# Two-block transformer on one core: softmax divided after the product with the values, and layer norms summed in groups

## The chip, the cores and the metric

One core of a Trainium2 chip runs the whole program in one launch. The metric is the device time in microseconds (us). The engines are named as in the profile: PE (TensorE, matrix products), DVE (VectorE), ACT (ScalarE), POOL (GpSimd) and SP (it issues the DMAs). PE works at one of two clock levels, 2.4 GHz (granted clock 1.0) or 1.2 GHz (0.5).

## What is computed

Two blocks follow each other on 512 positions of width 1024, each with two layers. The first block has feed-forward parts, a windowed attention and a recurrent mixer; the change leaves its attention alone. The second block has, in layer 0, multi-head latent attention ("MLA", 16 heads) and, in layer 1, neighbourhood attention ("NA", 16 heads). A stream of 256 context positions runs its own MLA beside the main one. All of it is float32. Cut to what matters:

```python
def layer_norm(x, g, b):
    mu = jnp.mean(x, -1, keepdims=True)
    var = jnp.mean(jnp.square(x - mu), -1, keepdims=True)
    return (x - mu) * lax.rsqrt(var + LN_EPS) * g + b

def dense_attention(...):          # MLA, per head and block of queries
    s = jnp.concatenate([q_ctx @ k_ctx, q_lat @ k_lat], -1)
    p = softmax_f32(s * scale)
    return p[..., :n_ctx] @ v_ctx + p[..., n_ctx:] @ v_lat
# NA: the same with a window of latent keys, a bias, and all context keys

h_lat = layer_norm(DEEPNORM_ALPHA * h_lat + g1 * y, ln1_g[i], ln1_b[i])   # after attention
h_lat = layer_norm(DEEPNORM_ALPHA * h_lat + g2 * f, ln2_g[i], ln2_b[i])   # after the feed-forward part
```

## The kernel before

The stream lies transposed: eight tiles `x[0]` to `x[7]` of 128 features by 512 positions. Each float32 factor of a big product is split into a high and a low part (`split`: an ACT copy and a DVE subtraction), and a product is three matmuls (`mm3`). Weights arrive by DMA as `wr` and are split into `wh` (ACT) and `wl` (DVE).

The order of the instructions is not the order of the Python text. All calls go to a `Recorder`; its `schedule` is a list scheduler that knows a cost for each operation and, engine by engine, picks the earliest recorded operation that is ready, within a look-ahead of 1400 operations. The whole program is then emitted in that order, one in-order queue for each engine. `run` mixes the context stream into the main one by a share of the planned PE time, and the modulation products (`mr`) by spare planned DVE time.

**Attention before.** `attend` (MLA) handles one head and 256 queries: scores to PSUM, the maximum, then the exponentials on ACT, which also add up the denominators `den`. DVE takes the reciprocal of the two columns of `den`, and POOL multiplies every weight tile by it through `times`: `pc` (two halves of 128x256, context keys) and, in the main stream, `pl` (two tiles of 128x512, latent keys). The function `output`, which `Lag` holds back by two units, transposes the weights on PE, splits them and multiplies them with the values. Then ACT and DVE put the two 64-row parts of the result together in `out` (tile `os`), which holds two heads; after the second head (`e` = 1) it is split into `yh`, `yl` for the output projection. There are 32 such units in the main stream (16 pairs of heads) and 16 in the context stream (8 pairs). The unit of `na` is a pair of heads on half the queries, 16 units: four reciprocals in one DVE instruction, four `times` on tiles `P` of 128x512, and later `na_out`.

**Norms before.** `ln_part` norms 256 positions at a time. `colsum` adds the eight tiles with `total` (seven additions in two chains) and then sums over the partitions by a matmul with ones for each 128 positions. The sums of `x` are added on POOL, those of the squares `sq` on DVE. Then come mean, variance, the row broadcasts by transposes (`ident,c`) and the scaling. `ln_part` runs ten times: twice for the context, twice (two halves) after each of MLA, feed-forward 0, NA and feed-forward 1. Of the latter the first half runs beside other PE work and the second half ends the stage.

In the trace the stages of the second block lie at about 2067 to 2370 us (MLA units), 2370 to 2400 (its norm), 2400 to 2815 (feed-forward 0), 2860 to 3192 (NA and its norm), 3192 to 3539 (feed-forward 1) and from 3539 on the last norm. The context MLA lies at 908 to 1350 us, inside the first block. Nearly all instructions carry line 446, which is the emitter's; they are told apart by their tiles.

Of the kernel before, what the change touches and what calls it, by code (L numbers as in the profile page):

```python
# [16 lines left out]
ALU = mybir.AluOpType  # L17
# [44 lines left out]
FIRST = (100, 16)  # L62
HEAVY = 0.5
FILL, DEBT, STEP = 0.7, 5000.0, 500.0
FIRST_POOL = (1, 3)
# [405 lines left out]
class Core:  # L471
# [254 lines left out]

    def colsum(self, tiles, T, eng=None, more=0):
        nc = self.nc
        acc = self.total(tiles, T, eng)
        st = self.ps()  # L730
        for j in range(T // P):
            nc.tensor.matmul(st[:, j:j + 1], acc[:, j * P:(j + 1) * P], self.ones, start=True, stop=True)
        n = T // P
        return st[:, :n] if not more else tuple(st[:, i * n:(i + 1) * n] for i in range(more + 1))
# [14 lines left out]
    def bcast(self, col, T, copy=None):  # L749
        bc = self.ps()  # L750
        for j in range(T // P):
            self.nc.tensor.transpose(bc[:, j * P:(j + 1) * P], col[:, j:j + 1].to_broadcast([P, P]), self.ident)
        if copy is None:
            return bc[:, :T]
        self.nc.scalar.copy(copy[:, :T], bc[:, :T])
        return copy[:, :T]

    def times(self, p, c):
# [453 lines left out]
    def ln_part(self, xs, T, l, which, kind, mod, perm=False):  # L1212
# [8 lines left out]
        def part(sl):  # L1221
# [9 lines left out]
            for a in x:  # L1231
                q = self.t(s="sq")[:, :C]
                nc.scalar.activation(q, a, AF.Square)
                sq.append(q)
            s1 = self.colsum(x, C, nc.gpsimd)
            s2, v, q = self.colsum(sq, C, more=2)
            mu, m2 = self.col(n), self.col(n)
# [60 lines left out]

    def attend(self, qs, kl, kc, vs, c0, yrow, e, scale, out):
        nc = self.nc  # L1300
# [19 lines left out]
        for j in range(2):  # L1320
            js = slice(j * 256, (j + 1) * 256)
            nc.scalar.activation(pc[:, js], sc[:, js], AF.Exp, bias=nm[:, j:j + 1], scale=scale, accum_out=den[:, j:j + 1])
            if nl:
                nc.scalar.activation(pl[j], pl[j], AF.Exp, bias=nm[:, j:j + 1], scale=scale, accum_out=den[:, 2 + j:3 + j])
        if nl:
            nc.vector.tensor_tensor(den[:, 0:2], den[:, 0:2], den[:, 2:4], op=ALU.add)
        nc.vector.reciprocal(den[:, 0:2], den[:, 0:2])
        for j in range(2):
            self.times(pc[:, j * 256:(j + 1) * 256], den[:, j:j + 1])
            if nl:  # L1330
                self.times(pl[j], den[:, j:j + 1])

        def output():
            o = self.ps("turn")[:, :256]
            prev = None
            for k2 in range(1 + nl // 2):
# [12 lines left out]
                prev = (k2, pt)  # L1349
            apply(o, *prev)  # L1350
            nc.scalar.copy(out[r], o[low])
            nc.vector.tensor_tensor(out[r], out[r], o[r], op=ALU.add)
            if e:
                self.split(out, [a[:, c0:c0 + 256] for a in yrow])

        def apply(o, k2, pt):
            for i in range(2):
                v = vs[0][i] if k2 == 0 else vs[1][(k2 - 1) * 2 + i]
                nc.group()
                for part, a in enumerate(pt):  # L1360
# [54 lines left out]
    def mla(self, a_lat, x, kind, ctx_only, ctx_kv, after):  # L1415
# [26 lines left out]
        for qd in range(4):  # L1442
# [16 lines left out]
            for pr in range(2):  # L1459
# [26 lines left out]
                for sl in parts(T):  # L1486
                    both = self.t(s="os")[:, :256]
                    for e in range(2):
                        vs = [[v[(hp % 4) // 2][:, ((hp % 2) * 2 + e) * P:((hp % 2) * 2 + e + 1) * P] for v in vt] for vt in vts]
                        yield from lag.add(self.attend(qs[e], kbl[e] if kbl else None, kbc[e], vs, sl.start, y, e, scale, both))  # L1490
                    if qd == 3 and pr:
                        yield from lag.add(lambda out=out, sl=sl: out(sl))
# [92 lines left out]

    def na_out(self, pts, vctx, vband, y, half):
        nc = self.nc
# [30 lines left out]
        for e in range(2):  # L1618
            rr = rows[e]
            nc.vector.tensor_tensor(ts[rr].rearrange("p (j q) -> p j q", j=2).sized(256), ts[rr].rearrange("p (j q) -> p j q", j=2),  # L1620
                                    o[rr].rearrange("p (j e q) -> p e j q", j=2, e=2)[:, e], op=ALU.add)
        src = ts.rearrange("p (c r) -> p c r", r=GRID_R)
        hv, lv = (b.rearrange("p (r c) -> p c r", c=GRID_W)[:, 32 * half:32 * half + 32, :].sized(256) for b in y)
# [3 lines left out]
    def na(self, x, a, after):  # L1627
# [11 lines left out]
        for pr in range(8):  # L1639
# [30 lines left out]
            for half in range(2):  # L1670
                pts = [[], []]
                den = self.col(4)
                for jj in range(2):
# [24 lines left out]
                yield from lag.add(lambda pts=pts, vctx=vctx, vband=vband, y=y, half=half: self.na_out(pts, vctx, vband, y, half))  # L1698
            ys.append(y)
# [142 lines left out]
```

## Time and profile before

| | |
|---|---|
| time, median of 3 runs | 3553.25 us (3552.89 to 3555.09) |
| the profiled execution | 3556.54 us |
| span of the profiled execution | 3554.8 us |
| PE busy | 3463.3 us (97%) |
| DVE busy | 2668.0 us (75%) |
| ACT busy | 1811.8 us (51%) |
| POOL busy | 768.6 us (22%) |
| chain that ended last | PE 88%, DVE 5%, ACT 3%, DMA 2% |

The profile is of one execution. Busy time is the union of the instructions' spans; a queued instruction can start before the one ahead has written its last element, so spans overlap. A wait is read from the idle time of an engine and from what released it. The chain that ended last is PE's in nearly all of the program: time is lost where PE is idle, and gained or spent where PE's own work changes.

### The profile page before, as it was taken

How to read it: one execution, taken by the hardware profiler on the slowest of the kernel's cores; microseconds unless marked ns; L12 is line 12 of the kernel's file. 1: busy time of each engine (PE TensorE's matmuls, PEld its weight loads, DVE VectorE, ACT ScalarE, POOL GpSimd, SP SyncE). 2: the span in 40 equal slices, each digit the busy share in tenths (PEclk: the TensorE clock that was granted, in tenths of full speed). 3: DMA queues.
4: the chain of work that ended last, by engine and by line, in shares of the span. 5: the costliest groups of instructions: out<-in, count | busy, mean ns of one | idle time of the engine just before them, and what ended most of it. 6: DMA issues, size and time to landing. Idle time of an engine off the chain costs nothing.

```text
span 3554.8 us, 56919 instructions
## 1 busy us (share of the span) xinstructions
PE 3463.3 (97%) x19814; PEld 3046.3 (86%) x19814; DVE 2668.0 (75%) x5556; ACT 1811.8 (51%) x3933; POOL 768.6 (22%) x848
## 2 busy tenths in 40 slices
PE   6999999999999999999999999999999999989998
PEld 5888989888988889898888988888888889988887
DVE  8984689867697658798645699987668767876566
ACT  6443555534555455664333487874445444454333
POOL 4330032322132112223100133350001522240002
PEclk9999999999999999999999999999999999999999
DMA  9874145556376542448535212124343143333330
GB/s 337 293 229 123 58 151 155 184 159 191 104 252 193 163 119 93 117 146 268 180 104 150 87 44 60 57 69 130 106 127 107 54 125 104 91 105 104 97 90 24
DMA packets 276448, 475.37 MB, mean 134 GB/s; under 512 B 40000, under 2 KB 55872, under 8 KB 276160
## 3 DMA queue, kind: packets, MB, share of 16 engines
q1 hardware_dynamic: 276160, 471.74, 43.4%
q8 instruction: 156, 2.56, 0.3%
q14 instruction: 132, 1.08, 0.1%
HBM read 448.81 MB, written 5.50 MB: 128 GB/s over the span
## 4 chain that ended last, share of the span: by engine, by line
PE 88%; DVE 5%; ACT 3%; DMA 2%; issue 1%; POOL 0%; SPq 0%; POOLq 0%; DVEq 0%; ACTq 0%
PE ps L446 88%; DVE wl L446 1%; ACT L446 1%; DVE c L446 0%; DVE x L446 0%; DVE pl L446 0%; ACT pth L446 0%; ACT pl L446 0%; SPq L446 0%; DMA mr<-in_wmod 0%; DVE ptl L446 0%; ACT gt L446 0%; DMA wr<-in_dn 0%; DVE mr L446 0%; ACT pc L446 0%
## 5 line engine op out<-in xcount | busy, mean ns | idle before, releaser
L446 DVE TENSOR_TENSOR wl<-wr,wh 128x512 fp32r<-128x512 f32 (+1 forms) x1182 | 851.9, 741 | 136.8 <-ACT wh L446 100.7
L446 ACT CAST wh<-wr 128x512 fp32r<-128x512 f32 (+1 forms) x1182 | 678.5, 614 | 116.6 <-PE ps L446 65.5
L446 PE MATMUL ps<-hh,wh 128*128 128x512 f32 (+1 forms) x1864 | 687.7, 369 | 4.9 <-ACT hh L446 4.8
L446 PE MATMUL ps<-hh,wl 128*128 128x512 f32 (+1 forms) x1864 | 684.5, 367 | 6.0 <-DVE wl L446 6.0
L446 PE MATMUL ps<-hl,wh 128*128 128x512 f32 (+1 forms) x1864 | 685.4, 368 | 4.4 <-DVE hl L446 4.4
L446 PE MATMUL ps<-fh,wh 128*128 128x512 f32 (+1 forms) x1344 | 464.1, 345 | 0.0
L446 PE MATMUL ps<-fl,wh 128*128 128x512 f32 (+1 forms) x1344 | 461.8, 344 | 0.0
L446 PE MATMUL ps<-fh,wl 128*128 128x512 f32 (+1 forms) x1344 | 461.7, 344 | 0.0
L446 PEld LDWEIGHTS ps<-hh,wl 128*128 128x128 f32 x1864 | 352.2, 189 | 65.6 <-DVE wl L446 7.8
L446 PEld LDWEIGHTS ps<-hh,wh 128*128 128x128 f32 x1864 | 352.6, 189 | 61.7 <-ACT hh L446 5.8
L446 PEld LDWEIGHTS ps<-hl,wh 128*128 128x128 f32 x1864 | 352.5, 189 | 61.2 <-DVE hl L446 6.4
L446 DVE SCALAR_TENSOR_TENSOR x<-ps,mods,x 128x512 f32<-128x512 f32 (+1 forms) x400 | 255.2, 641 | 177.8 <-PE ps L446 173.9
L446 PE MATMUL ps<-ah,wh 128*128 128x512 f32 (+1 forms) x1000 | 367.1, 367 | 2.0 <-ACT ah L446 2.0
L446 PE MATMUL ps<-al,wh 128*128 128x512 f32 (+1 forms) x1000 | 366.1, 366 | 0.2
L446 PE MATMUL ps<-ah,wl 128*128 128x512 f32 (+1 forms) x1000 | 365.7, 366 | 0.0
L446 PEld LDWEIGHTS ps<-fh,wl 128*128 128x128 f32 x1344 | 254.5, 189 | 30.2
L446 PEld LDWEIGHTS ps<-fh,wh 128*128 128x128 f32 x1344 | 254.6, 189 | 29.5
L446 PEld LDWEIGHTS ps<-fl,wh 128*128 128x128 f32 x1344 | 254.7, 190 | 29.3
L446 DVE SCALAR_TENSOR_TENSOR cv<-ps,ffc,cv 128x511 f32<-128x511 f32 (+1 forms) x264 | 172.6, 658 | 140.0 <-ACT cv L446 136.8
L446 POOL TENSOR_TENSOR mr<-mr,b_c 128x512 f32<-128x512 f32 x123 | 182.2, 1484 | 403.2 <-DMA mr<-in_wmod 287.8
L446 ACT ACTIVATE cv<-ps,ffc 128x512 f32<-128x512 f32 (+1 forms) x132 | 93.2, 708 | 323.5 <-PE ps L446 323.0
L446 ACT CAST fh<-s 128x512 fp32r<-128x512 f32 x132 | 81.9, 621 | 276.9 <-DVE s L446 276.9
(332 smaller groups left out, 6947.0 us busy)
## 6 DMA issues: line engine op xcount, KB each, us to landing
wr<-in_gu SPq DMA_DIRECT2D x352, 256.0 KB, 3.3
mr<-in_wmod SPq DMA_DIRECT2D x288, 256.0 KB, 4.4
wr<-in_fin SPq DMA_DIRECT2D x264, 256.0 KB, 2.7
mr<-in_wada SPq DMA_DIRECT2D x192, 256.0 KB, 3.6
wr<-in_dn SPq DMA_DIRECT2D x176, 256.0 KB, 3.1
wr<-in_fout SPq DMA_DIRECT2D x132, 256.0 KB, 2.7
wr<-in_win SPq DMA_DIRECT2D x64, 256.0 KB, 3.1
wr<-in_nqkv SPq DMA_DIRECT2D x48, 256.0 KB, 3.0
```

Source lines behind the costliest of these rows:

```text
L446: getattr(eng, method)(*a, **k)
```

## The change

The weights are no longer divided. `attend` writes its denominators into a tile `dn` of four columns, shared by two heads; `na` hands `den` to `na_out`. The reciprocals of the two-column and four-column denominators go, and so do all calls of `times` in MLA and NA (the first block's attention keeps its own). Instead a new function `rows2` takes, once for two heads, a reciprocal on DVE whose input is four columns repeated 64 times each, so the output `wide` (tile `dn`) is 128x256; two PE transposes turn it into rows in PSUM, and one DVE product multiplies the finished `os` by them. In MLA the transposes write the unused half of the bank of the product, in NA they take a bank of the kind `turn`.

The norms' sums of `ln_part` go in groups: of `x` the first six tiles are added on POOL and the tiles 6 and 7 go to PE as they are; of `sq` the first seven are added on DVE and the last goes to PE. PE adds the groups up in PSUM. The sums in `rms` stay.

```diff
+BY = ((6, 1, 1), (7, 1))
...
-    def colsum(self, tiles, T, eng=None, more=0):
...
-        acc = self.total(tiles, T, eng)
+    def colsum(self, tiles, T, eng=None, more=0, by=0):
...
+        accs, at = [], 0
+        for n in by or (len(tiles),):
+            accs.append(self.total(tiles[at:at + n], T, eng) if n > 1 else tiles[at])
+            at += n
         st = self.ps()
         for j in range(T // P):
-            nc.tensor.matmul(st[:, j:j + 1], acc[:, j * P:(j + 1) * P], self.ones, start=True, stop=True)
+            for i, acc in enumerate(accs):
+                nc.tensor.matmul(st[:, j:j + 1], acc[:, j * P:(j + 1) * P], self.ones, start=i == 0, stop=i == len(accs) - 1)
...
+    def rows2(self, out, c):
+        wide = self.t(s="dn")[:, :256]
+        self.nc.vector.reciprocal(wide.rearrange("p (c o) -> p c o", o=64).sized(256), c.rearrange("p (c o) -> p c o", o=1).to_broadcast([P, 4, 64]))
+        for j in range(2):
+            self.nc.tensor.transpose(out[:, j * P:(j + 1) * P], wide[:, j * P:(j + 1) * P], self.ident)
+        return out
...
-            s1 = self.colsum(x, C, nc.gpsimd)
-            s2, v, q = self.colsum(sq, C, more=2)
+            s1 = self.colsum(x, C, nc.gpsimd, by=BY[0])
+            s2, v, q = self.colsum(sq, C, more=2, by=BY[1])
...
-            nc.vector.tensor_tensor(den[:, 0:2], den[:, 0:2], den[:, 2:4], op=ALU.add)
-        nc.vector.reciprocal(den[:, 0:2], den[:, 0:2])
-        for j in range(2):
-            self.times(pc[:, j * 256:(j + 1) * 256], den[:, j:j + 1])
-            if nl:
-                self.times(pl[j], den[:, j:j + 1])
+            each = dn.rearrange("p (j e) -> p e j", e=2)[:, e].sized(2)
+            nc.vector.tensor_tensor(each, den[:, 0:2], den[:, 2:4], op=ALU.add)
...
+            if e:
+                per = self.rows2(bank[:, 256:], dn)
             nc.scalar.copy(out[r], o[low])
             nc.vector.tensor_tensor(out[r], out[r], o[r], op=ALU.add)
             if e:
+                nc.vector.tensor_tensor(out, out, per, op=ALU.mult)
                 self.split(out, [a[:, c0:c0 + 256] for a in yrow])
...
+        nc.vector.tensor_tensor(ts, ts, self.rows2(self.ps("turn"), den)[:, :256], op=ALU.mult)
         src = ts.rearrange("p (c r) -> p c r", r=GRID_R)
...
-                nc.vector.reciprocal(den, den)
-                for e in range(2):
-                    for jj in range(2):
-                        self.times(pts[e][jj], den[:, 2 * jj + e:2 * jj + e + 1])
```

The scheduler orders the whole program anew. The first place is DVE's queue late in MLA (`ptl` a split of transposed weights, `pl` scores with their maximum, `wl` a split of weights, `c` small columns, `yl` the split result). Before:

```order
L446 TENSOR_TENSOR c_26623<-c_26623 128x2
L446 SCALAR_TENSOR_TENSOR cv_26668<-ps_26470,ffc,cv_26668 128x255
L446 RECIPROCAL c_26623<-c_26623 128x2
L446 TENSOR_SCALAR pl_26692,c_26648<-ps_26653,c_26648 128x512
L446 TENSOR_TENSOR os_26563<-os_26563,ps_26591 64x256
L446 TENSOR_TENSOR ptl_26715<-ps_26651,pth_26682 128x512
L446 TENSOR_SCALAR pl_26723,c_26648<-ps_26664,c_26648 128x512
L446 TENSOR_TENSOR yl_26442<-os_26563,yh_26433 128x256
```

And of the changed kernel, DVE's queue at the same place in the program:

```order
L447 RECIPROCAL dn_26596<-c_26416 128x256
L447 TENSOR_REDUCE c_26608<-ps_26480 128x2
L447 TENSOR_TENSOR wl_26617<-wr_25715,wh_26015 128x512
L447 TENSOR_TENSOR c_26622<-c_26588 128x2
L447 TENSOR_SCALAR pl_26625,c_26608<-ps_26511,c_26608 128x512
L447 TENSOR_TENSOR os_26567<-os_26567,ps_26578 64x256
L447 TENSOR_SCALAR pl_26640,c_26608<-ps_26571,c_26608 128x512
L447 TENSOR_TENSOR os_26567<-os_26567,ps_26578 128x256
L447 TENSOR_SCALAR c_26643<-c_26608 128x2
L447 TENSOR_TENSOR wl_26645<-wr_26149,wh_26324 128x512
L447 TENSOR_TENSOR yl_26652<-os_26567,yh_26647 128x256
```

The small reciprocal has gone; a wide one stands ahead of the next unit's maximum and scores, and the product of `os` with the rows (128x256) stands between the sum of `os` and its split.

The second place is PE's queue at the last norm, the end of the program (`acc` a sum of tiles, `x_119` and `x_125` the tiles `x[6]` and `x[7]`, `ident,c` the two broadcasts). Before:

```order
L446 MATMUL ps_39566<-fh_39174,wl_38935 128x256
L446 MATMUL ps_39597<-ones,acc_39499 128x1 x2
L446 MATMUL ps_39600<-ones,acc_39506 128x1 x2
L446 MATMUL ps_39607<-ident,c_39602 128x128 x2
L446 MATMUL ps_39630<-ident,c_39611 128x128 x2
```

And in the changed kernel, PE's queue from the last product of the feed-forward part on:

```order
L447 MATMUL ps_39530<-fh_39134,wl_38895 128x256
L447 MATMUL ps_39554<-ones,acc_39445 128x1
L447 MATMUL ps_39554<-ones,x_119 128x1
L447 MATMUL ps_39558<-ones,acc_39451 128x1
L447 MATMUL ps_39554<-ones,x_125 128x1
L447 MATMUL ps_39554<-ones,acc_39445 128x1
L447 MATMUL ps_39554<-ones,x_119 128x1
L447 MATMUL ps_39554<-ones,x_125 128x1
L447 MATMUL ps_39558<-ones,sq_39560 128x1
L447 MATMUL ps_39558<-ones,acc_39451 128x1
L447 MATMUL ps_39558<-ones,sq_39560 128x1
L447 MATMUL ps_39573<-ident,c_39568 128x128 x2
```

Four matmuls with ones have become ten, and four of the sums of `x` stand behind the arrival of `x[7]`, where two POOL additions and all four matmuls stood.

The third place is DVE's queue at the last unit of NA. Before:

```order
L446 TENSOR_TENSOR ptl_35855<-ps_35827,pth_35843 128x512
L446 TENSOR_TENSOR os_35853<-os_35853,ps_35838 64x256 x2
L446 TENSOR_TENSOR wl_35873<-wr_35552,wh_35605 128x512
L446 TENSOR_TENSOR os_35853<-os_35853,ps_35858 64x256 x2
L446 TENSOR_TENSOR wl_35879<-wr_35561,wh_35619 128x512
L446 TENSOR_TENSOR wl_35882<-wr_35574,wh_35629 128x512
L446 TENSOR_TENSOR yl_35845<-os_35853,yh_35829 128x32x8
```

And in the changed kernel, DVE's queue for the same unit:

```order
L447 TENSOR_TENSOR ptl_35777<-ps_35747,pth_35763 128x512
L447 TENSOR_TENSOR os_35775<-os_35775,ps_35756 64x256 x2
L447 RECIPROCAL dn_35791<-c_35638 128x256
L447 TENSOR_TENSOR os_35775<-os_35775,ps_35771 64x256 x2
L447 TENSOR_TENSOR wl_35798<-wr_35118,wh_35159 128x512
L447 TENSOR_TENSOR os_35775<-os_35775,ps_35794 128x256
L447 TENSOR_TENSOR wl_35803<-wr_35128,wh_35165 128x512
L447 TENSOR_TENSOR wl_35806<-wr_35146,wh_35194 128x512
L447 TENSOR_TENSOR yl_35769<-os_35775,yh_35754 128x32x8
```

The wide reciprocal and the product have come into the last unit's way from the sums to the split.

In the whole program PE has 80 more transposes (`ident,dn`) and 60 more matmuls with ones, DVE 40 reciprocals of 128x256 and 40 products of 128x256 in place of 48 reciprocals of 128x2, 16 of 128x4 and 10 additions, and POOL 224 products and 20 additions fewer.

## Rows read from the trace of the kernel before

**Rows 1.** The page's first part: busy time of each engine.

```profile
PE 3463.3 (97%) x19814; PEld 3046.3 (86%) x19814; DVE 2668.0 (75%) x5556; ACT 1811.8 (51%) x3933; POOL 768.6 (22%) x848
```

**Rows 2.** Stretches: us; busy PE, PEld, DVE, ACT, POOL; granted clock; DMA share; GB/s.

```profile
2067.00:2370.00 303.00, 288.07 (x1962) 259.48 (x1960) 281.96 (x656) 253.90 (x614) 115.57 (x171) 1.00 0.19 56
2370.00:2400.00 30.00, 27.00 (x173) 26.00 (x173) 24.73 (x70) 17.35 (x44) 21.89 (x29) 0.78 0.36 109
...
2815.00:2860.00 45.00, 37.40 (x226) 33.08 (x225) 27.83 (x59) 17.84 (x37) 22.33 (x27) 0.92 0.47 123
2860.00:3110.00 250.00, 247.53 (x1698) 228.63 (x1697) 188.28 (x383) 123.44 (x284) 74.90 (x96) 1.00 0.38 101
3110.00:3192.00 82.00, 69.21 (x498) 65.65 (x497) 64.94 (x157) 42.56 (x99) 37.22 (x48) 0.90 0.31 95
...
3530.00:3554.80 24.80, 11.28 (x90) 10.44 (x88) 15.18 (x41) 6.70 (x14) 13.44 (x20) 0.78 0.26 85
908.00:1350.00 442.00, 442.00 (x2420) 385.13 (x2419) 319.03 (x654) 235.35 (x507) 86.89 (x91) 1.00 0.54 170
```

**Rows 3.** Groups of DVE in 2067 to 2370 us: count | busy us, mean ns | idle before.

```profile
L446 DVE TENSOR_TENSOR ptl<-ps,pth 128x512 fp32r<-128x512 f32 x96 | 63.4, 682 | 2.4 <-ACT pth L446 1.6
...
L446 DVE TENSOR_TENSOR os<-os,ps 64x256 f32<-64x256 f32 x32 | 13.3, 416 | 1.9 <-ACT os L446 1.0 <-POOL pl L446 0.2
...
L446 DVE TENSOR_TENSOR yl<-os,yh 128x256 fp32r<-128x256 f32 x15 | 7.4, 497 | 0.4 <-ACT yh L446 0.3
...
L446 DVE RECIPROCAL c<-c 128x2 f32<-128x2 f32 x32 | 5.1, 159 | 0.2
...
L446 DVE TENSOR_TENSOR f<-s,f 128x256 fp32r<-128x256 f32 x7 | 2.9, 420 | 0.0
```

**Rows 4.** PE's waits of the whole span: total us, times, longest.

```profile
PE ps L446 <- POOL P L446: 3.7, 4, 2.6
...
PE ps L446 <- POOL acc L446: 3.2, 2, 2.3
```

**Rows 5.** Groups of POOL in 2067 to 2370 us, columns as in Rows 3.

```profile
L446 POOL TENSOR_SCALAR pl<-pl,c 128x512 f32<-128x512 f32 x64 | 48.7, 761 | 0.0
L446 POOL TENSOR_SCALAR pc<-pc,c 128x256 f32<-128x256 f32 x64 | 35.8, 560 | 169.8 <-DVE c L446 85.9 <-ACT pc L446 22.8 <-ACT wh L446 21.0
```

**Rows 6.** Timeline of PE at NA's end: start, us, instruction, wait before.

```profile
3126.07 0.44 PE L446 MATMUL ps<-ident,P 128*128 128x128 f32 x2 [2.64 <-POOL P L446]
...
3134.64 1.42 PE L446 MATMUL ps<-ident,P 128*128 128x128 f32 x11 [0.34 <-POOL P L446]
...
3141.93 0.58 PE L446 MATMUL ps<-yh,wh 128*128 128x256 f32 x1 [2.11 <-ACT yh L446]
```

**Rows 7.** Timeline of the last norm, DVE: start, us, instruction, wait before.

```profile
3539.31 0.48 DVE L446 SCALAR_TENSOR_TENSOR x<-ps,mods,x 128x256 f32<-128x256 f32 x1 [0.51 <-PE ps L446]
...
3542.22 0.16 DVE L446 TENSOR_SCALAR c<-ps 128x2 f32<-128x2 f32 x1 [0.42 <-PE ps L446]
...
3546.97 2.74 DVE L446 TENSOR_TENSOR ln<-x,ps 128x256 f32<-128x256 f32 x8 [0.78 <-PE ps L446]
```

**Rows 8.** The matmuls with ones of the whole span, by form.

```profile
L446 PE MATMUL ps<-ones,acc 128*128 128x1 f32 x160 | 20.9, 243 | 15.0 <-DVE acc L446 11.8 <-POOL acc L446 3.2
```

**Rows 9.** Timeline of the last norm, PE.

```profile
3541.58 1.05 PE L446 MATMUL ps<-ones,acc 128*128 128x1 f32 x8 [2.31 <-POOL acc L446]
...
3546.24 0.69 PE L446 MATMUL ps<-ident,c 128*128 128x128 f32 x2 [3.34 <-DVE c L446]
```

**Rows 10.** The reciprocals of the whole span, by form.

```profile
L446 DVE RECIPROCAL c<-c 128x2 f32<-128x2 f32 x48 | 7.7, 160 | 8.1 <-ACT pc L446 7.7
L446 DVE RECIPROCAL c<-c 128x4 f32<-128x4 f32 x33 | 5.7, 172 | 1.8 <-ACT P L446 1.5
```

**Rows 11.** Timeline of the last norm, POOL.

```profile
3539.94 0.72 POOL L446 TENSOR_TENSOR acc<-acc,x 128x256 f32<-128x256 f32 x1 [1.42 <-DVE x L446]
3540.74 0.78 POOL L446 TENSOR_TENSOR acc<-acc,acc 128x256 f32<-128x256 f32 x1
```

More of the change, by code (lines that the diff above doesn't have):

```diff
@@ L1297, in spread, with attend @@
         return t
-    def attend(self, qs, kl, kc, vs, c0, yrow, e, scale, out):
+    def attend(self, qs, kl, kc, vs, c0, yrow, e, scale, out, dn):
         nc = self.nc
@@ L1321, in attend @@
             js = slice(j * 256, (j + 1) * 256)
-            nc.scalar.activation(pc[:, js], sc[:, js], AF.Exp, bias=nm[:, j:j + 1], scale=scale, accum_out=den[:, j:j + 1])
+            d = den[:, j:j + 1] if nl else dn[:, 2 * j + e:2 * j + e + 1]
+            nc.scalar.activation(pc[:, js], sc[:, js], AF.Exp, bias=nm[:, j:j + 1], scale=scale, accum_out=d)
             if nl:
@@ L1325, in attend @@
         if nl:
-            nc.vector.tensor_tensor(den[:, 0:2], den[:, 0:2], den[:, 2:4], op=ALU.add)
-        nc.vector.reciprocal(den[:, 0:2], den[:, 0:2])
-        for j in range(2):
-            self.times(pc[:, j * 256:(j + 1) * 256], den[:, j:j + 1])
-            if nl:
-                self.times(pl[j], den[:, j:j + 1])
+            each = dn.rearrange("p (j e) -> p e j", e=2)[:, e].sized(2)
+            nc.vector.tensor_tensor(each, den[:, 0:2], den[:, 2:4], op=ALU.add)
         def output():
-            o = self.ps("turn")[:, :256]
+            bank = self.ps("turn")
+            o = bank[:, :256]
             prev = None
@@ L1486, in mla @@
                 for sl in parts(T):
-                    both = self.t(s="os")[:, :256]
+                    both, dn = self.t(s="os")[:, :256], self.col(4)
                     for e in range(2):
                         vs = [[v[(hp % 4) // 2][:, ((hp % 2) * 2 + e) * P:((hp % 2) * 2 + e + 1) * P] for v in vt] for vt in vts]
-                        yield from lag.add(self.attend(qs[e], kbl[e] if kbl else None, kbc[e], vs, sl.start, y, e, scale, both))
+                        yield from lag.add(self.attend(qs[e], kbl[e] if kbl else None, kbc[e], vs, sl.start, y, e, scale, both, dn))
                     if qd == 3 and pr:
@@ L1584, in na_values, with na_out @@
         return [[(v01, 0), (v01, 256)], [(mid, 0), (mid, 256)], [(mid, 256), (end, 0)], [(v23, 0), (v23, 256)]], vc
-    def na_out(self, pts, vctx, vband, y, half):
+    def na_out(self, pts, den, vctx, vband, y, half):
         nc = self.nc
@@ L1693, in na @@
                         pts[e].append(pt)
-                nc.vector.reciprocal(den, den)
-                for e in range(2):
-                    for jj in range(2):
-                        self.times(pts[e][jj], den[:, 2 * jj + e:2 * jj + e + 1])
-                yield from lag.add(lambda pts=pts, vctx=vctx, vband=vband, y=y, half=half: self.na_out(pts, vctx, vband, y, half))
+                yield from lag.add(lambda pts=pts, den=den, vctx=vctx, vband=vband, y=y, half=half: self.na_out(pts, den, vctx, vband, y, half))
             ys.append(y)
```

## The prediction

> **What bounds the kernel now.** I read the page's first part, then the busy times by stretch, then the groups and waits inside the stretches that the change touches. The first part [rows 1] shows PE busy for 3463.3 of 3554.8 us: 91.5 us of idle time in all is the most that shorter waits can give, and work added to PE is paid wherever PE has no gap. The stretches [rows 2] are to be read by their idle time. In the context MLA (908 to 1350) PE has none. In the main MLA (2067 to 2370, 303 us) two engines are close to full: PE 288.07 (14.9 idle) and DVE 281.96 (21.0 idle). In NA up to 3110 PE has 2.5 us idle and DVE some 60; NA's end and its norm (3110 to 3192) have 12.8 us of PE idle. In DVE's groups of the main MLA [rows 3] the reader is to look at the idle time behind the second bar: 96 splits of `ptl` with 63.4 us of work waited 2.4 us in all. DVE has a queue there nearly all the time; it is as much the bound as PE. PE's waits [rows 4] say what POOL's products cost PE today: 3.7 us on `P`, 3.2 us on `acc`.
>
> **What goes.** POOL loses 224 products, 84.5 us of it in the main MLA [rows 5], where POOL is busy 115.57 of 303 us [rows 2]; PE's list of waits names POOL for `P` and `acc` alone. The 3.7 us on `P` all lie at the end of NA; the longest is 2.64 [rows 6]. So the removal is worth about 3.7 us there and close to nothing in MLA, since the unit's hand-over is covered by the two units that lag. POOL and DVE may also get into each other's way less. The 15 subtractions `yl` take 497 ns and the 7 `f` of the same form 420 [rows 3]; if that is POOL's doing, it is 1.2 us on `yl` alone, and I count 3 us for all of DVE in MLA, a choice. The 32 small reciprocals of the main MLA are 5.1 us of DVE [rows 3]. In a queue an instruction takes less than its span: eight `ln` of 128x256 take 2.74 us together [rows 7], 0.34 each, against 0.416 for one `os` of as many columns [rows 3]. So I take off 0.08 from each: 32 x 0.08 = 2.6 us.
>
> **What comes on PE.** A transpose takes 0.109 us: eleven take 1.42 us and two 0.44 [rows 6], so nine more take 0.98. 80 of them are 8.7 us: 1.7 in the context, 3.5 in the main MLA, 3.5 in NA. A matmul with ones counts twice: the trace has 160 rows [rows 8] for 80 in the program, and the four of the last norm are the x8 of its timeline [rows 9], 1.05 us; less the last one's span of 0.243 [rows 8] that is 0.807/7 = 0.115 for each row. The 60 new ones are therefore 120 rows, 13.8 us, 1.38 for each of the ten norm parts. Six of the ten run beside other PE work (two of the context, four first halves), 8.3 us to be paid in full. Four end a stage, where PE waits anyway.
>
> **What comes on DVE.** The wide reciprocal has no row. The nearest are the small ones [rows 10]: 160 ns for two columns, 172 for four, so 6 ns for each column more; 252 more columns make 1.51 us, 1.68 us in all. The lower bound is that it goes like other instructions of that width, 0.42 us. I take 1.68 because these rows are the same operation. The product with the rows is like `ln`, 0.34 in the queue. In the main MLA this is 16 x (1.60 + 0.34) = 31.0 us, less 2.6 and 3 from above: +25.4 us on an engine that had 21.0 us idle. 282 + 25.4 = 307.4 us is more than the whole stretch of 303; even without any wait it would grow by 4 us, and with today's idle time by 25. The order of the changed kernel has the same other work between the stage's first `pl` and last `yl`, so nothing has been moved out to make room. I take an idle share of 3% instead of 7%, as under more load the queue is emptier less often: 307.4/0.97 = 317, **+14 us**. It covers MLA's own 3.5 us of transposes, since PE then has slack.
> In the context MLA, DVE is busy 319.03 of 442, and 8 x 1.94 = 15.5 us fit into 123; in NA 31 us more fit into 78 (2860 to 3192) [rows 2]. Those I cost at nothing beside PE's part, except at NA's end: there a wide reciprocal and a product stand in the last unit's way to `yh`, for which PE already waits 2.11 us [rows 6]. The product is 0.34, the reciprocal 0 to 1.6, as it may fall into DVE's wait for PE: +1.6 in all.
>
> What the small rows say of one column, 6 ns, can be laid beside the Trainium skill: "VectorE: DVE Perf Modes", section "First, the fixed hardware budget", says that a reciprocal is a divide iterated with a repeat count of eight. Taken as eight plain columns that is an estimate of 8.3 ns a column; the rows' 6 ns lie below that and far above a plain instruction's column, and no run here yet shows a wide one. By the page the sum would be that of rival (2).
>
> **Norms at the ends.** Today at the last norm `x[7]` is there at 3539.79 (3539.31 + 0.48) [rows 7]; POOL adds it, then the two chains, until 3541.52 [rows 11], the matmuls start at 3541.58 [rows 9] and the mean at 3542.22 [rows 7]. With groups, PE takes `x[7]` at about 3539.9; four matmuls of `x` remain, eight rows, 0.9 us, and the mean starts near 3541.0: 1.2 us earlier. The square sums follow with three matmuls, 0.7 us, also about 1.1 us earlier than today. The rest of the chain, to `ident,c` at 3546.24 [rows 9], is unchanged. For four such ends I take 4 x 1.2 = **-4.8 us**; a wide reciprocal that stands ahead of the mean on DVE at MLA's norm may take one of them back.
>
> **The sum.** PE where it is covered by nothing: 1.7 (context) + 3.5 (NA) + 8.3 (norms) = 13.5. MLA +14. Norm ends -4.8. NA's waits -3.7 + 1.6 = -2.1. Together +20.6. The profiled execution took 3556.54 us (its span 3554.8), 3.3 above the median of 3553.25; on it the sum gives 3577, on the median **3574 us**, slower by 0.6%.
>
> **Rivals.**
> (1) DVE's new work is absorbed, so that POOL's leaving changes nothing but PE's work counts: the reciprocal goes like a plain instruction (16 x 0.68 = 11 us less 5.6, within the 21 idle), or the queue fills its gaps. MLA then costs PE's 3.5: 13.5 + 3.5 - 4.8 - 2.1 = +10, 3563. For it: 21 us of idle time; against it: the slope of the small reciprocals.
> (2) A column of the reciprocal takes eight times a plain one: that is 8 x (682 - 416)/256 = 8.3 ns by `ptl` and `os` [rows 3], 2.1 us for one. MLA's DVE work is then 282 + 16 x (2.02 + 0.34) - 5.6 = 314, at 3% idle 324, +21; in all +28, 3581. The slope of the small reciprocals speaks for something below it. [...]
> (3) Nothing is absorbed: the idle time in MLA are waits for ACT and PE that stay, and 1.6 us of a reciprocal ahead of `pl` or `ptl` starves PE. MLA +25: +32, 3585; with (2)'s price about 3593. In the stretch after MLA, where PE has gaps, the granted clock is 0.78 [rows 2], so PE spent a part of it at 1.2 GHz; longer gaps in MLA could bring the same there.
> (4) Faster: the hand-over exponential, reciprocal, four POOL products, transposes was what kept the attention stages short of work. If all PE idle time in them went (14.9 + 2.5 + 12.8 = 30.2) [rows 2], the sum is 22.5 for PE's work, less 30.2, less 4.8: -12.5, 3541. It decides from 29 us of saved idle time on, 22 for PE's work and 7 to be seen as faster; the waits on POOL are 6.9 us in all [rows 4], which speaks against it.
>
> **Chances.** My forecast 0.46, (1) 0.18, (2) 0.15, (3) 0.13, (4) 0.08. The order of the whole program is new, which can shift any of them by a few us. About 0.2%, 7 us, is what a measurement of this kernel can tell from no change. Faster by more than that: 0.07, nearly all of (4). Within it (3546 to 3560): 0.14, of which 0.10 from (1), the rest from the edges of the forecast and of (4). Slower: 0.79. The range leaves out (4) and the upper half of (3): 3557 to 3592.
>
> **What would show it.** In the changed profile: a wide reciprocal of 1.5 to 2.1 us, 40 of them; transposes of `dn` at 0.11; 280 rows of matmuls with ones; DVE above 96% busy in MLA and that stage some 14 us longer, while NA stays within 5 us; at the last norm 1.2 us less between `x[7]` and the mean. The forecast is wrong if MLA isn't longer although DVE got its 25 us, or if PE's idle time falls by more than 20 us.

## The result, and the profile after

| | before | after |
|---|---|---|
| median of 4 runs each, taken together | 3554.17 us | 3608.29 us (3604.76 to 3612.0) |
| ratio to before | 1 | 1.0148, 95% interval 1.0135 to 1.016 |
| the profiled execution | 3556.54 us | 3609.7 us |
| its span | 3554.8 us | 3607.9 us |

The changed kernel is 54 us (1.5%) slower: the direction of the forecast, more than twice its size, and 16 us above the upper end of its range.

The page's first part of the changed kernel, to be laid beside [rows 1]:

```profile
PE 3498.3 (97%) x20014; PEld 3076.8 (85%) x20014; DVE 2721.7 (75%) x5562; ACT 1810.4 (50%) x3930; POOL 603.0 (17%) x604
```

POOL lost 166 us of work, DVE gained 54, PE has 200 rows more. The time must be looked for by stage. Stretches of before first, from MLA's first latent score to its last `yl` and the same of NA (these bounds differ from those of [rows 2]), then of the changed kernel; columns as in [rows 2]:

```profile
2064.70:2370.00 305.30, 290.37 (x1976) 261.49 (x1974) 284.27 (x661) 255.76 (x618) 115.57 (x171) 1.00 0.19 56
2856.00:3142.40 286.40, 273.86 (x1854) 251.41 (x1854) 214.94 (x439) 145.98 (x334) 81.65 (x104) 0.99 0.41 111
```

```profile
2064.00:2393.00 329.00, 305.12 (x2002) 273.65 (x2000) 308.70 (x672) 261.89 (x633) 41.62 (x52) 0.96 0.16 51
...
2891.00:3196.00 305.00, 275.87 (x1856) 251.56 (x1856) 237.40 (x450) 143.42 (x328) 28.81 (x40) 0.98 0.37 100
```

The main MLA takes 329.0 us instead of 305.3, NA 305.0 instead of 286.4. In MLA, DVE's busy time rose by 24.4 us and its idle time stayed: 21.0 before, 20.3 after. In NA, DVE has 68 us to spare and PE lost time all the same; PE's idle time there went from 12.5 to 29.1 us. The granted clock fell from 1.00 to 0.96 in MLA.

DVE's groups in the changed kernel's MLA (2064 to 2393 us), columns as in [rows 3]:

```profile
L447 DVE TENSOR_TENSOR ptl<-ps,pth 128x512 fp32r<-128x512 f32 x96 | 62.9, 680 | 2.0 <-ACT pth L447 1.6
...
L447 DVE RECIPROCAL dn<-c 128x256 f32<-128x256 f32 x16 | 27.8, 1740 | 0.0
...
L447 DVE TENSOR_TENSOR os<-os,ps 64x256 f32<-64x256 f32 x32 | 13.3, 415 | 4.2 <-ACT os L447 3.7
...
L447 DVE TENSOR_TENSOR os<-os,ps 128x256 f32<-128x256 f32 x16 | 6.6, 414 | 0.2
```

```profile
L447 DVE TENSOR_TENSOR yl<-os,yh 128x256 fp32r<-128x256 f32 x15 | 6.1, 406 | 0.0
```

The wide reciprocal takes 1.74 us, 40 times in the program. `yl` fell from 497 ns [rows 3] to 406. In the kernel before, six of the 15 `yl` ran with no POOL instruction beside them and took 411 to 425 ns; of the nine that ran beside one, five took 550 to 742. In the changed kernel 14 of 15 have none beside them.

**Three parts of PE's time.** Since PE is the bound, I split each kernel's time from its first to its last matmul. *Work* is the count of matmuls of each form times the distance between two starts in an unbroken row at full clock (0.2265 us for 512 columns, 0.120 for 256, 0.109 for 128, 0.1125 for one). *Idle* is PE's idle time in the trace. The *rest* is what is left: matmuls at the lower clock, and the longer span of a matmul that stands ahead of a wait. In the profiled executions PE's time grew by 53.7 us: 22.2 of work, 18.6 of idle time and 12.8 of rest. Of the rest, 7.9 us are matmuls at the lower clock (counted in the stretches that the trace marks as such: 16.9 us before, 24.8 after). The table of all kernels stands behind the experiments.

The same split by stage, with idle time and rest together, gives +19.9 us in the main MLA and +20.9 in NA. The stretch between the two gives back 9.4 and the one behind NA 5.3; the part ahead of MLA loses 5.4. The new order also moves work from stage to stage (the stretch between MLA and NA holds 22 us more of it than before), so the lengths of the stages don't show by themselves where time was lost.

### The profile page after: what moved, and what is told of

It reads as the page before. It is cut to its first block, busy times and chain, and to the rows that moved or that the text cites. A ratio compares the mean times of both kernels' runs of the same rounds, so it can differ in the third digit from the quotient of the medians.

```text
span 3607.9 us, 56904 instructions
## 1 busy us (share of the span) xinstructions
PE 3498.3 (97%) x20014; PEld 3076.8 (85%) x20014; DVE 2721.7 (75%) x5562; ACT 1810.4 (50%) x3930; POOL 603.0 (17%) x604
## 3 DMA queue, kind: packets, MB, share of 16 engines
q14 instruction: 128, 1.05, 0.1%
## 4 chain that ended last, share of the span: by engine, by line
PE 87%; DVE 6%; ACT 4%; DMA 2%; issue 1%; SPq 0%; POOL 0%; POOLq 0%; DVEq 0%; ACTq 0%
PE ps L447 87%; DVE wl L447 1%; DVE x L447 1%; DMA kc<-kc 1%; ACT L447 1%; DVE c L447 1%; DVE ptl L447 1%; ACT pth L447 0%; ACT pl L447 0%; DVE mr L447 0%; DVE acc L447 0%; DVE dn L447 0%; DVE os L447 0%; ACT pc L447 0%; DMA qh<-ql 0%
## 5 line engine op out<-in xcount | busy, mean ns | idle before, releaser
L447 PEld LDWEIGHTS ps<-fl,wh 128*128 128x128 f32 x1344 | 254.7, 190 | 29.5
```

Source lines behind the costliest of these rows:

```text
L447: getattr(eng, method)(*a, **k)
```

## The experiments

Five theories are named in the expectations. A: the DVE time of the wide reciprocals makes the loss. B: any new order of the program brings it, whatever the reciprocal. C: the norms' part brings it. D: the order made for the reciprocal's planned price brings it ("smooth" where a higher price makes it worse step by step). E: each order is a random draw. The planner's price matters since the list scheduler simulates the engines with it; a wide reciprocal is planned at 65 + 6.3 x 256 = 1678 ns.

| run | median us | ratio to before, 95% interval |
|---|---|---|
| e1, norms' groups alone | 3562.53 | 1.0018 (1.0009 to 1.0027) |
| e2, attention alone | 3600.05 | 1.0125 (1.0108 to 1.0142) |
| e3, short reciprocal, the changed kernel's order | 3605.55 | 1.0138 (1.0123 to 1.0153) |
| e4, short reciprocal, planned at its own price | 3577.26 | 1.0057 (1.0042 to 1.0072) |
| e5, wide reciprocal in e4's order | 3601.14 | 1.0126 (1.0111 to 1.0141) |
| e6, short, planned at 0.9 us | 3580.04 | 1.0064 (1.0049 to 1.0079) |
| e7, short, planned at 0.5 us | 3579.46 | 1.0061 (1.0044 to 1.0078) |
| e8, wide, planned at 1.5 us | 3618.6 | 1.0174 (1.0159 to 1.0189) |
| e9, short, MLA alone | 3562.46 | 1.0022 (1.0013 to 1.0031) |
| e10, short, NA alone | 3564.86 | 1.0034 (1.002 to 1.0047) |
| e11, groups at the stages' ends alone | 3553.71 | 0.9998 (0.999 to 1.0007) |
| e12, before in another order | 3554.72 | 0.9994 (0.9985 to 1.0004) |

The kernel before, run beside each, had medians of 3554.56 to 3556.91 us.

### Which half of the change: e1 and e2

In e1 the attention is that of before, and only `colsum` and its two calls in `ln_part` are changed. In e2 it is the other way round, by one line:

```diff
-BY = ((6, 1, 1), (7, 1))
+BY = (0, 0)
```

> The kernel before with the norms' sums in groups and nothing else. Theory A (the wide reciprocals on DVE made the loss of 54 us): the norms cost PE 8.3 us where it is covered by nothing and give back 4.8 us at four stage ends, so 3558 us, +4 on before (0 to +8). Theory B (the new order of the whole program made the loss, whatever the pieces cost): any new order is as bad, so this one too lies 10 us or more from before, 3565 or more. Theory C (the norms made a good part of it): +20 or more.

> The changed kernel with the norms' sums as they were, the attention part alone. Theory A: 3604 us, +50 on before, all but the norms' 4 us, with MLA some 24 us and NA some 17 us longer than before. Theory B: anything between 3560 and 3610, with other stages bearing the loss. Theory C: 3585 or less.

e1 costs 6 us, e2 43 to 45; together they are near the 54 of the whole. Theory C falls as the main cause: the attention carries four fifths.

### The reciprocal's time and the order: e3, e4 and e5

The wide reciprocal is replaced by a reciprocal of the four columns and a copy that repeats each 64 times, grouped so that the planner counts them as one step. In e3 the planner is told the wide one's price, so that each engine's order is that of the changed kernel; in e4 it is told the copy's own price.

```diff
-        self.nc.vector.reciprocal(wide.rearrange("p (c o) -> p c o", o=64).sized(256), c.rearrange("p (c o) -> p c o", o=1).to_broadcast([P, 4, 64]))
+        nc.group()
+        nc.vector.reciprocal(c, c)
+        nc.vector.tensor_copy(wide.rearrange("p (c o) -> p c o", o=64).sized(256), c.rearrange("p (c o) -> p c o", o=1).to_broadcast([P, 4, 64]))
+        nc.group()
...
+            if method == "tensor_copy":
+                return 6.3 * (n - 4)    # e3
+                return 65 + 1.05 * n    # e4
```

> The changed kernel with each reciprocal of 128x256 (1.74 us) replaced by one of 128x4 and a copy that repeats it to 128x256, together about 0.5 us by the rows of before (0.17 and 0.34), planned at the wide one's price, so that every engine's order of instructions is the changed kernel's. Theory A: DVE gets 40 x 1.25 = 50 us back, of which MLA and NA have 16 x 1.25 = 20 us each; MLA falls by 15 to 20 us and NA by 12 to 17, the time to about 3575 (3568 to 3582). Theory B: order, and with it the waits on DMA at kc in NA, are unchanged: the time stays at 3595 or more.

> The same with the short pair planned at its own price of about 0.42 us, so that the scheduler makes a new order for it. Theory A: as the same-order run or a few us better, 3565 to 3578; PE's 22 us of added work remain and the kernel of before isn't beaten. Theory B: the order decides, so it differs from the same-order run by 15 us or more in either direction.

The pair costs 168 + 328 ns in place of 1743, by DVE's forms in e3's whole span (the 57 reciprocals are 40 of the pairs and 17 of the first block):

```profile
L449 DVE COPY dn<-c 128x256 f32<-128x256 f32 x40 | 13.1, 328 | 2.9 <-PE ps L449 0.6 <-issue 0.4
L449 DVE RECIPROCAL c<-c 128x4 f32<-128x4 f32 x57 | 9.6, 168 | 3.9 <-ACT pc L449 3.7
```

DVE lost 43 us of busy time in e3 (2678.5 against 2721.7), and the time fell by about 3, which the intervals don't tell from nothing. That is against theory A as I had put it. With the same instructions in the order that the true price gives (e4), the time is 28 us lower. Where the freed DVE time went in e3 is seen in its MLA stretch, to be laid beside the 329.00 above:

```profile
2063.00:2391.00 328.00, 304.48 (x2003) 273.46 (x2001) 291.59 (x688) 262.07 (x633) 41.74 (x52) 0.96 0.17 51
```

DVE is busy 17 us less, and idle 36.4 us instead of 20.3. What it waited for there, in the changed kernel and then in e3 (us, times, longest):

```profile
DVE c L447 <- ACT pl L447: 2.2, 5, 1.2
```

```profile
DVE c L449 <- ACT pl L449: 8.5, 11, 2.3
```

And PE's waits stand at the same instructions with nearly the same lengths: of 13 that exceed 0.6 us in either kernel between 2064 and 2400 us, twelve agree within 0.2 us. Three of them, from the timeline of PE in the changed kernel:

```profile
2246.91 0.51 PE L447 MATMUL ps<-cn,wh 128*128 128x256 f32 x2 [2.89 <-DVE x L447]
...
2386.72 0.66 PE L447 MATMUL ps<-ident,c 128*128 128x128 f32 x2 [1.40 <-DVE c L447]
...
2393.91 0.39 PE L447 MATMUL ps<-yl,wh 128*128 128x256 f32 x1 [3.64 <-DVE yl L447]
```

And in e3:

```profile
2244.98 0.50 PE L449 MATMUL ps<-cn,wh 128*128 128x256 f32 x2 [2.89 <-DVE x L449]
...
2384.53 0.66 PE L449 MATMUL ps<-ident,c 128*128 128x128 f32 x2 [1.40 <-DVE c L449]
...
2391.72 0.58 PE L449 MATMUL ps<-yl,wh 128*128 128x256 f32 x1 [3.63 <-DVE yl L449]
```

The first of them has no wide reciprocal in the 20 us before it. DVE works there through the scalings of eight tiles in a row (4.86 us) while the matmul at the head of PE's queue waits for the result:

```profile
2241.99 4.86 DVE L447 TENSOR_TENSOR x<-x,ps 128x512 f32<-128x512 f32 x8
```

Such a wait was put there by the order, and a faster reciprocal doesn't take it away. MLA is only 4 us longer in e3 than in e4, but e3 has less of PE's work in these stages: in idle time and rest together, of the profiled executions, it loses 6.5 us more than e4 in MLA, 12.3 more in NA and 5.2 more ahead of MLA, and all other stretches are within 1 us. That alone would speak for theory D, that only the order counts. e5 is the other half: the wide reciprocal itself, planned at 424 ns, in exactly e4's order (`also` books the columns as written, as the pair does):

```diff
-                return 65 + 6.3 * n
+                return 65 + 6.3 * n if n < 256 else 424.0
...
-        self.nc.vector.reciprocal(wide..., c...)
+        self.nc.vector.reciprocal(wide..., c..., also=[c])
```

> The fourth cell to the three of the changed kernel and the two short pairs: the reciprocals of 128x256 are real (1.74 us), but planned at the short pair's price of 0.42 us, so that every engine has the order of the replanned run (3577 us). Theory D (the order that the scheduler makes for a price of 1.68 us cost the 30 us, not DVE's time): 3577 to 3585. Theory A, weakened (DVE's time does count, but only in an order that is not already slow): 40 x 1.25 = 50 us of DVE work come back, 20 in each of MLA and NA, and the time is 3600 or more.

It costs 24 us against e4. One order, one difference in duration: here theory A holds. MLA in e4 and then in e5:

```profile
2063.80:2387.80 324.00, 302.25 (x2027) 272.46 (x2026) 295.73 (x695) 263.40 (x636) 40.63 (x52) 0.98 0.18 55
```

```profile
2064.30:2408.20 343.90, 309.86 (x2016) 276.90 (x2015) 314.36 (x678) 264.75 (x636) 40.89 (x52) 0.96 0.17 51
```

The stage is 19.9 us longer, as much as 16 x (1.743 - 0.496) = 20.0: in sum the reciprocals are paid in full, and DVE's idle time is 28.3 us in one, 29.5 in the other. Only 12.3 of the 19.9 us are idle time of PE; the other 7.6 are longer busy time, with a granted clock of 0.96 in place of 0.98. The loss is spread over the units: at the same matmul PE is 0.5 us behind e4 ahead of the stage, 9.1 at 2200 us and 17.7 at 2350. In NA it is 4.6 us for 16 reciprocals, a quarter of their time, in e4 and then in e5:

```profile
2870.00:3167.60 297.60, 279.77 (x1886) 256.08 (x1886) 222.28 (x473) 146.51 (x334) 30.39 (x40) 0.98 0.39 107
```

```profile
2889.00:3191.20 302.20, 280.70 (x1886) 255.59 (x1886) 239.72 (x457) 146.62 (x334) 30.76 (x40) 0.98 0.39 105
```

The eight wide reciprocals of the context MLA cost next to nothing: PE is 0.3 us behind e4 ahead of them (880 us) and 0.5 behind them (1360 us). How a reciprocal reaches PE is seen at one place, the timelines of DVE and PE in e4:

```profile
2074.94 0.17 DVE L449 RECIPROCAL c<-c 128x4 f32<-128x4 f32 x1
2075.22 0.29 DVE L449 COPY dn<-c 128x256 f32<-128x256 f32 x1
2075.43 0.68 DVE L449 TENSOR_TENSOR wl<-wr,wh 128x512 fp32r<-128x512 f32 x1
2076.08 0.75 DVE L449 TENSOR_SCALAR_CACHE_REDUCE pl<-ps,c 128x512 f32<-128x512 f32 x1
...
2076.90 0.50 PE L449 MATMUL ps<-cnh,wh 128*128 128x512 f32 x1 [0.41 <-DVE pl L449]
```

And the same instructions in e5:

```profile
2075.48 1.75 DVE L447 RECIPROCAL dn<-c 128x256 f32<-128x256 f32 x1
2077.14 0.63 DVE L447 TENSOR_TENSOR wl<-wr,wh 128x512 fp32r<-128x512 f32 x1
2077.69 0.74 DVE L447 TENSOR_SCALAR_CACHE_REDUCE pl<-ps,c 128x512 f32<-128x512 f32 x1
...
2078.49 0.51 PE L447 MATMUL ps<-cnh,wh 128*128 128x512 f32 x1 [1.46 <-DVE pl L447]
```

DVE has no gap before `pl` in either. PE's next matmul waits until the scores' bank has been read by `pl`, so the reciprocal's extra 1.2 us comes out as 1.05 us more of waiting.

### Is it a random draw: e6, e7, e8 and e12

e6 and e7 are e4 with other planned prices for the pair (90.2 ns of it are the reciprocal's); e8 is the changed kernel with 1.5 us planned for the wide reciprocal. e12 is the kernel before with all its instructions, and the small reciprocals planned 235 ns too high, which reorders every queue.

```diff
+            if method == "tensor_copy":
+                return 900.0 - 90.2    # e6
+                return 500.0 - 90.2    # e7
...
+                return 65 + 6.3 * n if n < 256 else 1500.0    # e8
...
-                return 65 + 6.3 * n
+                return 300 + 6.3 * n    # e12
```

> The short pair (0.5 us on DVE) planned at 0.9 us, halfway between 0.42 (3577 us) and 1.68 (3606). Theory D, smooth (a higher price makes a slower order step by step): 3585 to 3597. Theory E (each new order is a draw with a spread of some 10 us, whatever the price): anywhere from 3565 to 3610, and not between the two for a reason.

> The short pair planned at 0.50 us in place of 0.42, a change that means nothing. Theory D, smooth: 3577 to 3581. Theory E: 3565 to 3595, as far from 3577 as the other orders are from each other.

> The changed kernel with its reciprocals planned at 1.50 us in place of 1.68, a change that means little (they take 1.74). Theory D, smooth: 3602 to 3610. Theory E: 3575 to 3615; if it lies 15 us or more below the changed kernel, a part of the 54 us is the draw of one order.

> The kernel before, with not one instruction changed; only the planner's price of a small reciprocal is 235 ns higher than it is, so the list scheduler gives the whole program another order. This measures what an order alone is worth here. Theory E (each order of this program is a draw, and the one of before a lucky one): 5 to 15 us slower than before, 3559 to 3569; then the 8 us that attention on NA alone cost beyond PE's work, and part of every other run's difference, needs no cause of its own. Theory D (only an order made for a large wrong price is slow): within 4 us of before, 3550 to 3558, as 48 reciprocals of 235 ns too much are 11 us of planned DVE time against 64 us for the wide ones; then what the runs above show beyond PE's work comes from the attention's new steps.

The three short versions lie within 3 us of each other (3577 to 3580), the three wide ones between 3601 and 3619, and before doesn't change in another order (ratio 0.9994). Theory D in its smooth form falls: it wanted 3585 to 3597 for e6, and e8 lies above both its range and that of theory E. Theory E falls as an explanation of 20 us or more for the kernels without the wide reciprocal: an order alone is worth some 3 us where the plan's price is within 0.4 us of the instruction's time. It stays open for the wide versions, whose orders differ by up to 17 us; the one that was planned with a price far too low (e5) is the best of them. That an order made for the wide reciprocal is slow in itself rests on a single such order, that of e3.

e12 says one thing more. Its NA (from the first context score to the last `yl`) takes 7.4 us longer than that of before, with the same work of PE, and the stretch from MLA's first latent score to there 5.9 less. So a stage's own difference of some 7 us to before shows nothing by itself.

### The parts of the short version: e9, e10 and e11

e9 has the short pair in MLA alone (the context's too), e10 in NA alone, both with the norms of before. e11 has the attention of before, and the norms' groups only in the four parts that end a stage:

```diff
+            last = T == S and sl.start
-            s1 = self.colsum(x, C, nc.gpsimd, by=BY[0])
-            s2, v, q = self.colsum(sq, C, more=2, by=BY[1])
+            s1 = self.colsum(x, C, nc.gpsimd, by=BY[0] if last else 0)
+            s2, v, q = self.colsum(sq, C, more=2, by=BY[1] if last else 0)
```

> The kernel before with the new way in both MLA stages alone (24 units, reciprocals in the short form, planned at 0.42 us); NA divides by POOL as before, the norms are as before. PE gets 48 transposes, 5.2 us. If PE's work is all that remains once the reciprocal is short: +5 us, 3561 to 3565. If the product with the rows (0.34 us on DVE, 16 times) is paid in full in the main MLA as well: +10, 3565 to 3570. If POOL's leaving helps MLA: below 3557.

> The kernel before with the new way in NA alone (16 units, short form). PE gets 32 transposes, 3.5 us. By the step of the prediction (the waits on POOL at NA's end go, 3.7 us, the product costs 0.3): 0 to +2, 3556 to 3559. If NA's length in the short-reciprocal runs (297 to 299 us from the first score to the last split, before 286) comes from NA's own part of the change: +8 to +12, 3564 to 3569, with the waits on POOL replaced by waits on ACT for the exponentials.

> The kernel before with the sums in groups only in the second halves that end a stage (four of the ten norm parts). If the groups everywhere (+6 us) are PE's 8.3 us in six covered parts less what the four ends give back: this one keeps the gain alone, -2 to -5 us, 3552 to 3555. If the ends give nothing: 3556 to 3560.

MLA alone costs 8 us, NA alone 10, the ends nothing that can be told from zero (-0.9 us, interval -3.6 to +2.5). None is faster than before. NA alone is the odd one, with 3.5 us of PE work. In its profiled execution NA is 8.0 us longer (3.5 of work, 3.4 idle, 1.0 rest), and each other stage is within 1 us of before. Its waits of PE in that stage (2850 to 3150 us), us, times, longest:

```profile
PE ps L449 <- ACT P L449: 4.4, 6, 1.5
PE ps L449 <- DVE ptl L449: 3.8, 8, 1.1
PE ps L449 <- ACT yh L449: 3.0, 1, 3.0
```

The 3.7 us on POOL's `P` [rows 4] are gone, and 4.4 us on the exponentials that write the same `P` (0.6 before) have come in their place. So the loss lies in NA. Whether the part beyond PE's work comes from the new steps or from NA's new order stays open, since in e12 an order alone moved NA by as much.

### All runs by PE's three parts

| kernel | time of PE | work | idle | rest |
|---|---|---|---|---|
| before | 3535.4 | 3413.3 | 72.1 | 50.0 |
| e12, before, another order | 3531.1 | 3413.3 | 72.0 | 45.8 |
| e11, ends alone | 3533.4 | 3418.7 | 66.3 | 48.4 |
| e9, short, MLA alone | 3538.3 | 3418.5 | 72.7 | 47.1 |
| e10, short, NA alone | 3542.1 | 3416.8 | 72.0 | 53.3 |
| e1, norms alone | 3543.6 | 3426.8 | 66.5 | 50.4 |
| e4, short | 3560.6 | 3435.5 | 69.6 | 55.5 |
| e6, short, planned at 0.9 | 3553.9 | 3435.5 | 70.9 | 47.5 |
| e7, short, planned at 0.5 | 3559.5 | 3435.5 | 71.2 | 52.8 |
| e2, attention alone, wide | 3572.6 | 3422.0 | 92.0 | 58.5 |
| e3, short in the wide one's order | 3583.3 | 3435.5 | 82.9 | 65.0 |
| e5, wide in the short one's order | 3584.3 | 3435.5 | 87.0 | 61.8 |
| after | 3589.0 | 3435.5 | 90.7 | 62.8 |
| e8, wide, planned at 1.5 | 3598.5 | 3435.5 | 95.3 | 67.8 |

This is the answer in one view. Without the wide reciprocal, and in an order made without it, PE's idle time and rest are in sum close to those of before, and the kernel is slower by about PE's own new work, 22.2 us. With the wide reciprocal, or in the order made for it, 11 to 23 us of idle time and 12 to 18 us of rest come on top.

That the sum of the short versions is so close to PE's work is in part luck. By stage, e4 loses 12 us beyond its work in MLA and 7 in NA, and gains 9 in the stretch between them and 6 behind NA. The parts don't each cost their work either: 8 us for 5.2 of work in the two MLA parts (e9), 10 for 3.5 in NA (e10), 6 for 13.5 in the norms (e1).

## Why the prediction was wrong

The direction and the prices of the new work were right. Three steps failed: DVE's idle share in MLA, taken at 3% and measured at 6.2%; NA, put at nothing beside PE's part and 17.6 us longer; and the lower clock, which had no price and took 7.9 us.

**PE's new work: right.** 22.5 us were forecast and 22.2 counted. The forms after, from the listing of the tile `ones` (duration in ns, first and last start):

```profile
L447 PE MATMUL ps<-ones,acc x160: 164/250/371, 11.3 to 3595.4; 128*128 128x1 f32 x160
...
L447 PE MATMUL ps<-ones,x x64: 168/250/271, 2374.1 to 3594.9; 128*128 128x1 f32 x64
...
L447 PE MATMUL ps<-ones,sq x40: 168/250/250, 1426.4 to 3595.6; 128*128 128x1 f32 x40
...
L447 PE MATMUL ps<-ones,hc x16: 250/250/250, 1415.8 to 2757.4; 128*128 128x1 f32 x16
```

160 + 64 + 40 + 16 (the context's tiles are named `hc`) are the 280 rows of the forecast.

**What hides PE's new work: right at the ends, wrong in MLA.** I let MLA's 3.5 us of transposes vanish in PE's slack and the 5.5 us at four norm ends in its waits. At the ends they do vanish: e11 has 5.4 us more work and is no slower (-0.9 us). In MLA nothing is seen to vanish: e9, with 5.2 us of transposes in the two MLA parts, is 8 us slower.

**The reciprocal's price: right.** 1.743 us against 1.68: 6.2 ns a column between the 128x4 and the 128x256 form. The Trainium skill, "VectorE: DVE Perf Modes", section "First, the fixed hardware budget", gives the repeat count of eight and no time for a column; read as eight plain columns it made an estimate of 2.1 us. The measured one is 1.743, so the measurement decides, and rival (2) fell.

**DVE's new work in MLA: right in amount, wrong in what becomes of it.** DVE's busy time there rose by 24.4 us, forecast 25.4. The step that failed is "I take an idle share of 3% instead of 7%": it was 6.2% (20.3 of 329.0), so the stage grew by 23.7 us and not by 14. That was rival (3)'s mechanism, with +25 for MLA. I had read the 21 us of idle time as slack that a longer queue would fill. e5 shows that DVE's gaps stay as long as they were (28.3 and 29.5 us in one order) while the 16 reciprocals are paid in full in sum, at places such as the one at 2075 us, where DVE has no gap and PE waits for the instruction behind. e3 adds that the order that expects the long reciprocal loses the time in another way: its waits stay when the reciprocal is short. In the context MLA the forecast held: the eight long reciprocals, which were to fit into DVE's 123 us of idle time, cost PE 0.3 us (e5 against e4).

**NA: wrong.** "Those I cost at nothing beside PE's part", within 5 us. From its first context score to its last `yl` it is 17.6 us longer (304.1 against 286.5; the window of the changed kernel shown above is 0.9 us wider), and its idle time and rest grew by 20.9. DVE has room there, and I concluded from that that PE would not notice. PE's waits in NA, of the kernel before (2856 to 3142.4 us) and then of the changed one (2891 to 3196 us; `kc` are the context keys, "issue" is time for which the trace names nothing):

```profile
PE ps L446 <- DMA kc<-kc: 3.2, 3, 1.5
```

```profile
PE ps L447 <- DMA kc<-kc: 8.6, 7, 1.6
PE ps L447 <- issue: 4.7, 2, 2.8
PE ps L447 <- ACT P L447: 4.5, 6, 1.6
PE ps L447 <- DVE ptl L447: 4.4, 7, 1.6
PE ps L447 <- DVE dn L447: 2.9, 2, 1.8
```

POOL is no longer in this list, as forecast, but the gain did not follow. The longest entry is now the load of `kc`, 5.4 us more than before, and that is not the reciprocal's doing alone: it is 6.9 in e12, which has the instructions of before, and 5.9 in e3. By e5 the wide reciprocal's share of NA is about 5 us, by e12 up to some 7 may be the order's; the rest is not told apart.

**The norms' ends: right at the last one, worth less in sum.** The last norm of the changed kernel, DVE and then PE, to be laid beside [rows 7, 9]:

```profile
3593.57 0.48 DVE L447 SCALAR_TENSOR_TENSOR x<-ps,mods,x 128x256 f32<-128x256 f32 x1 [0.31 <-PE ps L447]
3595.19 0.16 DVE L447 TENSOR_SCALAR c<-ps 128x2 f32<-128x2 f32 x1 [1.15 <-PE ps L447]
...
3600.41 2.74 DVE L447 TENSOR_TENSOR ln<-x,ps 128x256 f32<-128x256 f32 x8 [0.78 <-PE ps L447]
```

```profile
3599.68 0.69 PE L447 MATMUL ps<-ident,c 128*128 128x128 f32 x2 [3.34 <-DVE c L447]
```

From `x[7]` (3594.05) to the mean are 1.14 us, before 2.43: 1.3 saved, forecast 1.2. To the broadcasts it is 5.63 against 6.45, so 0.8 is left. In the whole (e11) four such ends give -0.9 us with an interval down to -3.6, where I had put -4.8: PE's idle time is 5.8 us less, and the new matmuls take 5.4 of it.

**The lower clock: missing.** I had named it only under rival (3), without a price. It is 7.9 us of the 53.7, a seventh of the loss, within 12.8 us of rest; of e5's 24 us against e4, 17.4 are idle time and 6.3 the rest.

**The range.** It ended at 3592 since rival (3) was counted with MLA alone. Its +25 there is close to the 23.7 measured; its own mechanism would have had to be applied to NA as well, where the sum has +1.4 (3.5 of PE's work, -2.1 of waits) and the runs 17.6. With that, its +32 would have been near +48, against 54 measured; since the new order moves work between the stages, this is a rough account. Rival (4) had nothing for it: no run shows a gain from POOL's leaving.

## What to carry to other kernels

Idle time on an engine with an in-order queue is not by itself a reserve that new work can fill: ask of each new instruction what stands behind it in that queue and who waits for that. In one order, longer reciprocals were paid in full where DVE in e4 was busy for 91% of the stage (main MLA), by a quarter at 75% (NA) and hardly at all at 69% (context MLA). Take the reciprocal of the narrow operand and repeat it by a copy (0.50 us here) rather than of the repeated one (1.74 us). With a planner that orders by prices, test a new instruction's cost with the order held fixed as well as replanned, since here the order made for a long instruction stayed slow when the instruction had become short. And when a kernel is slower by just as much as its new work, look at the parts before calling all of it paid: here it was a sum of larger losses and gains.

## What the runs showed of the hardware that I had not expected

A wait of PE can cost more than itself. After the 2.89 us of idle time that end at 2246.91 us in the changed kernel, the granted clock of PE in the stretch around it and in the one behind was:

```profile
2246.00:2251.00 5.00, 4.09 (x18) 3.82 (x19) 4.83 (x13) 1.69 (x4) 0.00 (x0) 0.66 0.14 38
2251.00:2257.00 6.00, 6.00 (x51) 5.86 (x50) 4.51 (x9) 5.13 (x14) 2.54 (x4) 1.00 0.13 44
```

0.66 is a mean of the two levels. In the timeline of the same place matmuls of 512 columns start 0.41 to 0.42 us apart at first and 0.24 apart from 2250.90 on:

```profile
2250.07 0.63 PE L447 MATMUL ps<-cnl,wh 128*128 128x512 f32 x1
2250.49 0.57 PE L447 MATMUL ps<-cnh,wl 128*128 128x512 f32 x1
2250.90 0.40 PE L447 MATMUL ps<-cnh,wh 128*128 128x512 f32 x1
2251.14 0.39 PE L447 MATMUL ps<-cnl,wh 128*128 128x512 f32 x1
```

Here this echo, what the matmuls up to 2250.9 us took beyond full clock, is 1.7 us. It does not follow every wait: after 2.01 us of idle time that end at 2316.54 us in the same kernel, the granted clock of the next 5 us is 1.00. Between PE's first and last matmul the stretches at the lower level add up to 44 us before and 66 after; the matmuls in them take 16.9 us more than at full clock before and 24.8 after, so the difference is 7.9 of the 12.8 us by which the rest grew. The wait itself is listed; its echo stands in no list of waits, only in the granted clock.
